# Input projection on a fixed five-engine order, and an output projection 512 columns wide, in a three-mixer decoder layer

## The chip, the cores and the metric

The kernel runs on one core of a Trainium2 chip. The metric is the device time of one execution in microseconds, the median of several runs; lower is better. Engines are named as in the profile: PE (TensorE matmul) and PEld (its weight load), DVE (VectorE), ACT (ScalarE), POOL (GpSimd), SP (SyncE, here only a queue that issues DMAs).

## The reference

One decoder layer, SEQ 1024, D_MODEL 1024, all in float32 (cut to what matters here):

```python
ada = silu(c) @ w_ada + b_ada
sh1, sc1, g1, sh2, sc2, g2 = split(ada, 6)
xn = modulate(rmsnorm(x, norm1), sh1, sc1)
z = xn @ w_in
a_u, a_v, b_x, b_g, c_q, c_k, c_v, z_gate = split(z)
out_a = gelu(a_u) * spatial_gating(layernorm(gelu(a_v)))
out_b = rg_lru(causal_conv(b_x)) * gelu(b_g)
out_c = dilated_attention(c_q, c_k, c_v)
gates = sigmoid(z_gate)
merged = gates[0] * (out_a @ p_a) + gates[1] * (out_b @ p_b) + gates[2] * (out_c @ p_c)
x = x + g1 * (merged @ w_out)
x = x + g2 * ffn(modulate(rmsnorm(x, norm2), sh2, sc2))
out = rmsnorm(x, final_norm)
```

a_u, a_v, b_x, b_g, c_q, c_k and c_v are 768 columns wide each, z_gate 3072. w_in therefore has 8448 columns.

## The kernel before

Every float32 product is made of three float32r matmuls: a high part and a low part of both operands, and of the four products the one of the two low parts is left out. The high part of a weight tile is a copy that rounds, on ACT (L116), the low part a subtraction (L117) on DVE or POOL. The projection works with a two by two block scheme of seven products instead of eight (`ORDER`): each product multiplies one of A11, A12, S1 to S4, A22 (blocks or sums of blocks of the weights) with one of B11 to T4 (blocks or sums of the activations, made once), and adds to one of four PSUM banks x, y, z and w. Three of the products use bank x and two bank z, in this order: A11 to x, A12 to y, S1 to z, S2 to x, S3 to x, A22 to w, S4 to z. Behind A11, S2 and S3 ACT copies x out (L161, L165, L167); DVE adds or subtracts behind A12, S3, A22 and S4 (L163, L168, L170, L172).

A **unit** (`unit_ws`, L176 to L194, matmul L191) makes two blocks of 128 output columns for all 1024 tokens: seven products of 12 matmuls of 512 columns. There are 25 units in the stretch of the profile that is called the projection here: one for the last two blocks of b_x, three each for b_g, a_u, c_q and c_k, twelve for the gates. c_v and a_v are made token by token row (`project_rows`, matmul L266): three units of 14 half-products of 24 matmuls of 256 columns. Four sums of weights per unit (S1 to S4, L148) alternate between POOL and DVE, and so do the low parts.

Between the units the code issues **side work** that needs their results: bias tables for attention (`bias_tables`, L595), the RG-LRU (`recurrence`, six tiles; matmuls L650, sigmoids L651), spatial gating (`spatial_gating`, six tiles; matmuls L709, L715), the head copies and stores of q and k (`post_q`, `post_k`; copies L754 and L766), and twelve late quarters of the ada vector (`late`). Loads of this work stand on SP's queue among those of the weights. The order on each engine is not that of the code: the program is built with a scheduler that simulates a timeline and places instructions by it, from all units and side work at once.

Later, after attention, the merge multiplies the mixers' outputs with p_a, p_b, p_c and the gates (L1106, with L1110 and L1111 on DVE), and w_out follows in two halves of 512 tokens, each in four chunks of 256 columns; for each chunk, four groups of 24 matmuls run one after another, each in one PSUM bank (L1145), and DVE multiplies with g1 and adds x (L1148, L1149). Then the second norm, its transposes and the FFN follow, for which the same `unit_ws` is used.

## Time and profile before

| | |
|---|---|
| runs | median of 3: 2006.84 us (2004.11 to 2011.18) |
| profiled execution | 2004.11 us, span of its instructions 2002.4 us, mean granted TensorE clock 0.98 |
| PE, DVE, ACT, POOL busy | 94%, 65%, 45%, 43% of the span |
| set-up, to 92.7 us | ada, norm, activation blocks |
| projection with its side work | 92.7 to 829.9 us |
| attention and merge | to 1224.3 us |
| w_out | to 1319 us |
| FFN and final norm | to the end |

The profile comes from one execution. A line number with L is a line of the kernel. "Idle before <- X" is the time in which an engine stood still ahead of an instruction, and what ended it. The granted clock is the clock that TensorE was given in a stretch, as a share of 2.4 GHz; its other level is 1.2 GHz. A matmul's record is longer than the distance to the next one, since matmuls are pipelined.

### The profile page before, as it was taken

What the parts mean: (1) busy time and instruction counts of PE and PEld (TensorE: products, weight loads), DVE (VectorE), ACT (ScalarE), POOL (GpSimd) and SP (SyncE); (2) the same over time, 40 slices, a digit from 0 to 9 for tenths busy, and PEclk for the clock granted to TensorE, in tenths of its full rate; (3) what the DMA queues carried; (4) which work ended last, traced back from release to release, by engine and by line L of the source; (5) the groups of instructions that cost most, each with busy time, mean ns of one, the idle gap of its engine ahead of it and who ended that gap; (6) DMA issues with size and microseconds to landing.
All of it is one profiled execution on the core that took longest, in us unless ns stands there. A gap on an engine that the chain in (4) does not pass through costs nothing. (4 is left out here: it accounts for less than half of the span.)

```text
span 2002.4 us, 27413 instructions
## 1 busy us (share of the span) xinstructions
PE 1887.5 (94%) x9503; PEld 1535.3 (77%) x9503; DVE 1300.0 (65%) x2171; ACT 896.7 (45%) x1638; POOL 857.1 (43%) x1133
## 2 busy tenths in 40 slices
PE   6889999899898989999899999998999999999997
PEld 5658998667676767778778777986787887877886
DVE  5776566477645764455556767669867666656787
ACT  5246456463643334544444433345443443334544
POOL 5453445355354334244655666456444444400002
PEclk9899999999998999999999999999999999999999
DMA  9232344347877654877876545422424333467674
GB/s 317 74 117 93 127 135 149 101 143 224 273 222 208 202 166 145 233 180 172 192 164 166 150 139 209 132 90 76 156 97 143 119 100 111 142 245 235 218 225 176
DMA packets 269994, 328.66 MB, mean 164 GB/s; under 512 B 17583, under 2 KB 196899, under 8 KB 269856
## 3 DMA queue, kind: packets, MB, share of 16 engines
q1 hardware_dynamic: 228848, 213.97, 36.0%
q10 hardware_dynamic: 33744, 87.18, 12.2%
q0 software_dynamic: 7264, 25.77, 5.2%
q8 instruction: 74, 1.21, 0.3%
q14 instruction: 64, 0.52, 0.1%
HBM read 238.64 MB, written 88.22 MB: 163 GB/s over the span
## 5 line engine op out<-in xcount | busy, mean ns | idle before, releaser
L191 PE MATMUL g<-xs,wh 128*128 128x512 f32 x2520 | 807.8, 402 | 41.9 <-DVE ot L168 11.1
L191 PEld LDWEIGHTS g<-xs,wh 128*128 128x128 f32 x2520 | 477.1, 191 | 169.6 <-DVE ot L168 12.8
L191 PE MATMUL g<-xs,wl 128*128 128x512 f32 x1260 | 499.7, 399 | 0.1
L117 POOL TENSOR_TENSOR wl<-st,wh 128x512 fp32r<-128x512 f32 x153 | 239.5, 1568 | 312.5 <-ACT wh L116 285.3
L116 ACT ACTIVATE wh<-raw 128x512 fp32r<-128x512 f32 (+2 forms) x341 | 202.1, 607 | 353.7 <-PE g L191 88.9
L191 PEld LDWEIGHTS g<-xs,wl 128*128 128x128 f32 x1260 | 239.8, 190 | 59.5 <-issue 3.4
L117 DVE TENSOR_TENSOR wl<-raw,wh 128x512 fp32r<-128x512 f32 (+2 forms) x240 | 186.5, 783 | 120.0 <-ACT wh L116 119.6
L116 ACT ACTIVATE wh<-st 128x512 fp32r<-128x512 f32 x215 | 133.4, 628 | 264.4 <-PE g L191 168.2
L117 POOL TENSOR_TENSOR wl<-raw,wh 128x512 fp32r<-128x512 f32 (+2 forms) x101 | 137.0, 1358 | 171.4 <-ACT wh L116 160.9
L148 POOL TENSOR_TENSOR st<-raw 128x512 f32<-128x512 f32 x102 | 156.6, 1539 | 119.4 <-DVE wl L117 90.6
L888 PE MATMUL gp<-oT,wh 128*128 128x512 f32 x512 | 169.7, 412 | 0.9 <-DVE ot L172 0.9
L266 PE MATMUL g<-wh,xs 128*128 128x256 f32 x672 | 126.1, 288 | 0.0
L958 ACT ACTIVATE pm<-pm,stat 128x128 f32<-128x128 f32 (+1 forms) x192 | 89.0, 465 | 51.6 <-DVE stat L955 51.1
L266 PEld LDWEIGHTS g<-wh,xs 128*128 128x128 f32 x672 | 105.0, 190 | 3.8 <-issue 3.7
L888 PEld LDWEIGHTS gp<-oT,wh 128*128 128x128 f32 x512 | 89.4, 191 | 21.8 <-issue 9.0
L1353 PE MATMUL g<-wh,wl 128*128 128x512 f32 x264 | 104.3, 395 | 0.0
L1353 PE MATMUL g<-wl,wh 128*128 128x512 f32 x264 | 104.2, 395 | 0.0
L1371 POOL TENSOR_TENSOR ms<-ms 128x1 f32<-128x1 f32 x8 | 3.6, 446 | 235.1 <-ACT junk L1370 235.0
L888 PE MATMUL gp<-oT,wl 128*128 128x512 f32 x256 | 101.9, 398 | 0.0
L1353 PE MATMUL g<-wh 128*128 128x512 f32 x264 | 94.1, 395 | 8.2 <-ACT wh L116 8.2
L266 PE MATMUL g<-wl,xs 128*128 128x256 f32 x336 | 95.4, 284 | 0.0
L955 DVE CUSTOM_DVE_ANT_0 pm<-sl,bt 128x128 f32<-128x128 f32 (+1 forms) x192 | 64.0, 378 | 47.8 <-PE sl L950 47.8
(296 smaller groups left out, 3454.1 us busy)
## 6 DMA issues: line engine op xcount, KB each, us to landing
raw<-in_w_in_dram SPq DMA_DIRECT2D x66, 512.0 KB, 5.0
raw<-in_f_wdown_dram SPq DMA_DIRECT2D x77, 256.0 KB, 5.6
adaw<-in_w_ada_dram SPq DMA_DIRECT2D x48, 256.0 KB, 6.0
g_scr<-ot ACTq DMA_DIRECT2D x24, 512.0 KB, 3.8
raw<-in_w_ada_dram SPq DMA_DIRECT2D x24, 512.0 KB, 3.6
qk<-q_scr POOLq DMA_DIRECT2D x12, 1024.0 KB, 6.4
qk<-k_scr POOLq DMA_DIRECT2D x24, 512.0 KB, 10.1
raw<-g_scr SPq DMA_DIRECT2D x24, 512.0 KB, 3.5
```

The costliest lines, as they stand in the source:

```text
L116: act.activation(h, src, AF.Copy)
L117: l_eng.tensor_tensor(l, src, h.bitcast(F32), op=OP.subtract)
L148: engs[int(name[1]) - 1].tensor_tensor(s_, src.get(x_) if isinstance(x_, str) else x_, src.get(y_) if isinstance(y_, str) else y_, op=op)
L191: pe.matmul(banks[bk], a[:, k, :], b, start=(fresh and j == 0), stop=(j == 11), skip_group_check=True)
L266: pe.matmul(banks[t2][bk][:, 256 * i:256 * i + 256], a[:, sl], b[:, k % 2, :], start=(fresh and i == 0 and j == 0), stop=(j == 11), skip_g ...
L888: pe.matmul(pt, a_[:, k % g, :], b_, start=(j == 0), stop=(j == 3 * n - 1))
L955: dve.tensor_tensor_reduce(out=pm[:, of:of + n], in0=sb[:, of:of + n], in1=bt[:, cfg, 256 - n:], scale=1.0, scalar=3e38, op0=OP.add, op1=O ...
L958: act.activation(pm[:, of:of + n], pm[:, of:of + n], AF.Exp, scale=-1.0, bias=stt[:, cfg, 0, idx:idx + 1], accum_out=stt[:, cfg, 1, idx:id ...
L1353: pe.matmul(bank, a_[:, sl], b_, start=(start and j == 0), stop=(j == 2), skip_group_check=True)
L1371: pool.tensor_tensor(ms[:, 0:1], ms[:, 0:1], ms[:, 1:2], op=OP.add)
```

## The change

From the three b_g units on, the projection is written as a fixed order for all five engines (the scheduler is switched off for PE, ACT, DVE, POOL and SP up to the end of the projection). A **slot** is one product (for the token-row units one half-product). The class `Stream` sorts all steps by slot: a unit's weights are loaded 12 slots ahead (`LOAD`), the sum and the high part are made 5 slots ahead (`LA`), the low part 4 slots ahead (`LB`), then come the slot's matmuls (L295), then one step of each of two queues of side work (`feed`), which are now generators that yield between steps, then the evacuation. The addition behind S3 comes one slot after ACT's copy. All low parts and all sums of weights are on DVE (L258, L252), the high parts on ACT (L254). The loads of side work go from SP's queue to POOL's. The first tap of the recurrence's convolution and its square move from DVE to ACT, the low parts of k from POOL to DVE. The late ada vectors are made in 48 steps of 512 columns with three buffers of their own (96 steps of 256 before). The gate units are placed between the others, so that side work has units to go along with. w_out has two chunks of 512 columns with the loop over k outside and four PSUM banks side by side, in a pool of their own. The core of the diff:

```diff
+    LA, LB, LOAD = 5, 4, 12
+
+    class Unit:
...
+            def first():
+                bl = blocks()
+                if name in formed:
+                    x_, op, y_ = formed[name]
+                    bl[name] = ring_tmp(shape)
+                    dve.tensor_tensor(bl[name], bl[x_], bl[y_], op=op)
+                it["h"] = ring.tile([P] + shape, F32R, tag="wh", bufs=8, name="wh")
+                act.activation(it["h"], bl[name], AF.Copy)
+
+            def second():
+                it["l"] = ring.tile([P] + shape, F32R, tag="wl", bufs=8, name="wl")
+                dve.tensor_tensor(it["l"], blocks()[name], it["h"].bitcast(F32), op=OP.subtract)
...
+    def evac_steps(wn, banks, m0, m1):
+
+        if wn == "S3":
+            act.activation(m1[0], banks["x"], AF.Copy)
+            z_ = banks["z"]
+            return [(1, lambda: dve.tensor_tensor(m1[1], z_, m1[0], op=OP.add))]
+        unit_evac(wn, banks, m0, m1)
+        return []
...
+    def feed(*queues):
+        for q in queues or (side, rest):
+            while q:
+                if next(q[0], StopIteration) is not StopIteration:
+                    break
+                q.popleft()
+
+    class Stream:
...
+        def add(self, u):
+            for it in u.items:
+                it["pos"] = self.n + it["rel"]
+            self.todo += [(max(0, self.n - LOAD), 0, u.load)]
+            self.todo += [(max(0, it["pos"] - LB), 1, it["second"]) for it in u.items]
+            self.todo += [(max(0, it["pos"] - LA), 0 if it["pos"] < LA else 2, it["first"]) for it in u.items]
+            self.todo += [(self.n + i, 3, mm) for i, (mm, _) in enumerate(u.slots)]
+            self.todo += [(self.n + i, 5, evac) for i, (_, evac) in enumerate(u.slots)]
+            self.n += len(u.slots)
...
+        for i in range(3):
+            fetch(i)
+        for _ in range(3):
+            yield
+        for i, (a, h, k) in enumerate(order):
+            fetch(i + 3)
...
+    phase(["bt"], lambda: side.append(bias_tables(side_pool["bt"])))
+    for j in (0, 2):
+        stream.add(project(COL["bg"], z_scr["bg"], AF.Gelu_apprx_tanh, j))
+    phase(["rg"], queue_recurrence)
+    stream.add(project(COL["bg"], z_scr["bg"], AF.Gelu_apprx_tanh, 4))
+    for j in range(3):
+        stream.add(project_rows(j))
+        gate_units(2 * j)
+    for j in range(0, KW, 2):
+        stream.add(project(COL["au"], z_scr["au"], AF.Gelu_apprx_tanh, j))
+    phase(["sg"], lambda: side.append(spatial_gating(side_pool["sg"])))
+    gate_units(6, 8, 10, 12, 14, 16)
+    phase(["hl", "ad"], lambda: rest.append(late(side_pool["ad"])))
+    for name in "qk":
+        for j in range(0, KW, 2):
+            stream.add(project_heads(name, j, lambda: side_pool["hl"]))
+    gate_units(18, 20)
...
-            for c in range(4):
-                cs = slice(256 * c, 256 * c + 256)
...
-                for i in range(4):
-                    pt = gbank("go")
...
+            for c in range(2):
+                cs = slice(HALF * c, HALF * c + HALF)
+                pts = [pwo.tile([P, HALF], F32, tag="wo", bufs=4, name="go") for _ in range(4)]
+                for k in range(KD):
...
+                    for i, pt in enumerate(pts):
                         sl = slice(i * P, i * P + P)
+                        for j, (a_, b_) in enumerate(((mh, wh), (mh, wl), (ml, wh))):
+                            pe.matmul(pt, a_[:, sl], b_, start=(k == 0 and j == 0), stop=(k == KD - 1 and j == 2))
+                for i, pt in enumerate(pts):
+                    tmp = ring_tmp([HALF])
+                    dve.tensor_tensor(tmp, pt, g1b[:, cs], op=OP.mult)
                     dve.tensor_tensor(x2[i][:, cs], x2[i][:, cs], tmp, op=OP.add)
```

How instructions now stand, at three places. The first is PE's order in the projection around a unit's products S2 and S3, which share a bank (here a `g` with one number). Before, in the spatial gating's stretch: S2 ends in bank g_4540, then two matmuls into another unit's bank, two of side work (L709), and a product of a third unit (g_4412); S3's first matmul into g_4540 stands 18 rows behind S2's last.

```order
L191 MATMUL g_4540<-xs_1010,wh_4593 128x512
L191 MATMUL g_4540<-xs_1009,wl_4594 128x512
L191 MATMUL g_4540<-xs_1017,wh_4593 128x512
L191 MATMUL g_4540<-xs_1018,wh_4593 128x512
L191 MATMUL g_4540<-xs_1017,wl_4594 128x512
L191 MATMUL g_4634<-xs_1039,wh_4630 128x512 x2
L709 MATMUL m_4141<-vs_4128,wst_4124 128x512
L709 MATMUL m_4144<-vs_4128,wst_4124 128x512
L191 MATMUL g_4412<-xs_882,wh_4484 128x512
L191 MATMUL g_4412<-xs_883,wh_4484 128x512
```

Now, at the corresponding stretch, S2's last matmuls into g_4972, two of side work (L884, the same matmuls as L709), and S3's first ones into g_4972. 23 units have this order; in 13 of them nothing stands between S2 and S3, in the others one side step as here.

```order
L295 MATMUL g_4972<-xs_1009,wl_4943 128x512
L295 MATMUL g_4972<-xs_1017,wh_4914 128x512
L295 MATMUL g_4972<-xs_1018,wh_4914 128x512
L295 MATMUL g_4972<-xs_1017,wl_4943 128x512
L884 MATMUL m_5077<-vs_4933,wst_5052 128x512
L884 MATMUL m_5080<-vs_4933,wst_5052 128x512
L295 MATMUL g_4972<-xs_1023,wh_4947 128x512
L295 MATMUL g_4972<-xs_1024,wh_4947 128x512
L295 MATMUL g_4972<-xs_1023,wl_4968 128x512
```

What moved: the other unit's product that stood between the two is gone, so S3 follows the copy of the bank (L165) directly.

The second is ACT's order in the recurrence, ahead of L165. Before, L165 stood between splits, and the recurrence's activations (L651, L654, L655) behind it:

```order
L565 ACTIVATE ot<-ot 128x1024
L116 ACTIVATE wh<-st 128x512
L165 ACTIVATE ot<-g 128x512
L560 DMA au_scr<-ot 128x1024
L116 ACTIVATE wh<-raw 128x512
L651 ACT_TABLE_LOAD
L651 ACTIVATE rr<-m,cols_382 128x512 x2
L654 ACT_TABLE_LOAD
L654 ACTIVATE aa<-rr,spn 128x1024
```

Now (L789 is the same sigmoid as L651, L254 the split's high part, L677 a gelu of a finished unit):

```order
L254 ACTIVATE wh<-raw 128x512
L789 ACT_TABLE_LOAD
L789 ACTIVATE rr<-m,cols_382 128x512 x2
L254 ACTIVATE wh<-raw 128x512
L789 ACTIVATE ii<-m,cols_382 128x512 x2
L165 ACTIVATE ot<-g 128x512
```

What moved: a step of the recurrence stands directly ahead of L165. Three units have it so.

The third is PE's order where the merge ends and w_out begins. Before, the merge's groups (L1106) all end before the first matmul of w_out (L1145):

```order
L1106 MATMUL gp_11478<-oT_10995,wh_11278 128x512
L1106 MATMUL gp_11478<-oT_10996,wh_11278 128x512
L1106 MATMUL gp_11478<-oT_10995,wl_11279 128x512
L1145 MATMUL go_11538<-wh_11520,mh_11226 128x256
L1145 MATMUL go_11538<-wl_11521,mh_11226 128x256
L1145 MATMUL go_11538<-wh_11520,ml_11227 128x256
```

Now (L1370 is the merge, L1407 w_out, with its four banks go_11500 to go_11503):

```order
L1370 MATMUL gp_11313<-oT_10971,wh_11245 128x512
L1370 MATMUL gp_11313<-oT_10970,wl_11246 128x512
L1407 MATMUL go_11500<-wh_11506,mh_11205 128x512
L1407 MATMUL go_11500<-wl_11507,mh_11205 128x512
L1407 MATMUL go_11501<-wh_11506,mh_11205 128x512
L1407 MATMUL go_11501<-wl_11507,mh_11205 128x512
L1407 MATMUL go_11502<-wh_11506,mh_11205 128x512
L1407 MATMUL go_11502<-wl_11507,mh_11205 128x512
L1407 MATMUL go_11503<-wh_11506,mh_11205 128x512
L1407 MATMUL go_11503<-wl_11507,mh_11205 128x512
L1370 MATMUL gp_11325<-oT_10258,wh_11251 128x512
L1370 MATMUL gp_11325<-oT_10259,wh_11251 128x512
```

What moved: w_out's matmuls begin between the last groups of the merge.

## Rows read from the trace of the kernel before

**Rows 1.** Page, part 1: busy us, share of the span, instructions

```profile
PE 1887.5 (94%) x9503; PEld 1535.3 (77%) x9503; DVE 1300.0 (65%) x2171; ACT 896.7 (45%) x1638; POOL 857.1 (43%) x1133
```

**Rows 2.** By stage: window, us; busy (x) of PE, PEld, DVE, ACT, POOL; clock, DMA, GB/s

```profile
92.70:831.00 738.30, 686.84 (x3302) 551.35 (x3301) 458.28 (x619) 355.12 (x494) 321.94 (x256) 0.97 0.53 165
...
1224.30:1319.00 94.70, 94.70 (x792) 94.70 (x793) 53.89 (x87) 30.75 (x51) 38.97 (x35) 1.00 0.47 162
1319.00:1400.00 81.00, 76.49 (x352) 61.87 (x350) 70.50 (x67) 40.60 (x68) 51.89 (x41) 1.00 0.22 68
```

**Rows 3.** PE groups of the projection: x count, busy us, mean ns, idle before

```profile
L191 PE MATMUL g<-xs,wh 128*128 128x512 f32 x1400 | 458.7, 409 | 32.4 <-DVE ot L168 11.1 <-ACT ot L165 9.0 <-ACT wh L116 5.7
...
L650 PE MATMUL m<-xv,bd 128*128 128x512 f32 x48 | 25.6, 641 | 5.9 <-DVE xv L644 4.0 <-ACT rr L651 1.9
...
L950 PE MATMUL sl<-qk 128*128 128x256 f32 (+1 forms) x8 | 1.1, 280 | 0.0
```

**Rows 4.** Timeline of PE at full pace: start us, us

```profile
744.01 0.63 PE L191 MATMUL g<-xs,wh 128*128 128x512 f32 x2
...
744.72 0.63 PE L191 MATMUL g<-xs,wh 128*128 128x512 f32 x2
```

**Rows 5.** Timeline of PE: four of the 20 idles of 0.6 us and more

```profile
105.80 0.97 PE L191 MATMUL g<-xs,wh 128*128 128x512 f32 x3 [2.29 <-ACT xs L116]
...
640.93 1.22 PE L191 MATMUL g<-xs,wh 128*128 128x512 f32 x2 [5.69 <-ACT wh L116]
...
666.49 0.73 PE L191 MATMUL g<-xs,wh 128*128 128x512 f32 x2 [2.16 <-ACT ot L165]
...
826.80 0.73 PE L191 MATMUL g<-xs,wh 128*128 128x512 f32 x2 [2.82 <-DVE ot L168]
```

**Rows 6.** Granted clock around two of these idles (columns as in rows 2)

```profile
636.00:647.00 11.00, 6.07 (x16) 4.99 (x17) 5.44 (x5) 4.47 (x8) 5.92 (x5) 0.56 0.70 229
665.00:669.00 4.00, 2.51 (x11) 2.06 (x12) 2.12 (x4) 2.70 (x4) 1.40 (x1) 1.00 0.47 142
```

**Rows 7.** Split and sum groups of the projection on POOL and DVE

```profile
L117 POOL TENSOR_TENSOR wl<-st,wh 128x512 fp32r<-128x512 f32 x90 | 136.0, 1516 | 181.8 <-ACT wh L116 159.5 <-PE m L709 12.2 <-DMA q_scr<-ot 10.0
...
L148 POOL TENSOR_TENSOR st<-raw 128x512 f32<-128x512 f32 x59 | 92.9, 1580 | 68.3 <-DVE wl L117 40.8 <-DMA raw<-in_w_in_dram 21.6 <-DVE st L148 1.4
...
L117 DVE TENSOR_TENSOR wl<-raw,wh 128x512 fp32r<-128x512 f32 (+1 forms) x63 | 57.6, 915 | 46.9 <-ACT wh L116 46.9
...
L117 POOL TENSOR_TENSOR wl<-raw,wh 128x512 fp32r<-128x512 f32 (+1 forms) x33 | 49.2, 1493 | 81.9 <-ACT wh L116 77.1 <-DMA oT<-oa_scr 4.7
```

**Rows 8.** Line L117, whole kernel: ns min/median/max, first and last start

```profile
L117 DVE TENSOR_TENSOR wl<-st,wh x62: 671/683/1789, 83.0 to 1954.5; 128x512 fp32r<-128x512 f32 x62
```

**Rows 9.** Timelines of PE and ACT around the idle at 666.49

```profile
663.94 0.39 PE L191 MATMUL g<-xs,wl 128*128 128x512 f32 x1
...
665.32 0.63 ACT L116 ACTIVATE wh<-st 128x512 fp32r<-128x512 f32 x1 [2.85 <-DVE st L148]
665.85 0.58 ACT L165 ACTIVATE ot<-g 128x512 f32<-128x512 f32 x1
```

**Rows 10.** Head copies of the projection's q units on ACT

```profile
L766 ACT ACTIVATE hlp<-ot 128x1024 f32<-128x1024 f32 x6 | 12.4, 2070 | 8.9 <-issue 5.2 <-DMA q_scr<-hlp 3.7
```

**Rows 11.** Timeline of ACT at a table load

```profile
426.34 1.28 ACT L654 ACT_TABLE_LOAD   x1
...
427.64 1.15 ACT L654 ACTIVATE aa<-rr,spn 128x1024 f32<-128x1024 f32 x1
```

**Rows 12.** Timeline of PE at the merge's end: first and last of three idles

```profile
1214.90 0.73 PE L1106 MATMUL gp<-oT,wh 128*128 128x512 f32 x2 [1.71 <-DVE st L1110]
...
1222.56 0.74 PE L1106 MATMUL gp<-oT,wh 128*128 128x512 f32 x2 [1.70 <-DVE st L1110]
```

**Rows 13.** Page, part 6: DMA issues, KB each, us from issue to landing

```profile
adaw<-in_w_ada_dram SPq DMA_DIRECT2D x48, 256.0 KB, 6.0
...
qk<-k_scr POOLq DMA_DIRECT2D x24, 512.0 KB, 10.1
```

More of the change, by code (lines that the diff above doesn't have):

```diff
@@ new lines, in evac_steps, with stream_ws, blocks, mm @@
+    def evac_steps(wn, banks, m0, m1):
[5 more added lines that the diff above has]
+        return []
+    def stream_ws(gb, tcomb, views, ot, post):
+        u = Unit(views, [KD, P])
+        bl, banks, out_ = {}, {}, []
+        def blocks():
+            if not bl:
+                (r0, r1) = u.raws
+                bl.update(A11=r0[:, :4, :], A12=r0[:, 4:, :], A21=r1[:, :4, :], A22=r1[:, 4:, :])
+            return bl
+        for i, (wn, tn, bk) in enumerate(ORDER):
+            it = u.part(i, wn, blocks, [4, P])
+            def mm(wn=wn, tn=tn, bk=bk, it=it):
+                fresh = bk not in banks
+                if fresh:
+                    banks[bk] = gb(bk)
+                j = 0
+                for k in range(4):
+                    th, tl = tcomb[tn][k]
+                    for a, b in ((it["h"], th), (it["h"], tl), (it["l"], th)):
+                        pe.matmul(banks[bk], a[:, k, :], b, start=(fresh and j == 0), stop=(j == 11),
+                                  skip_group_check=True)
+                        j += 1
+            def evac(wn=wn):
+                if not out_:
+                    out_.extend(ot())
+                m0, m1 = out_
+                later = evac_steps(wn, banks, (m0[:, 0], m0[:, 1]), (m1[:, 0], m1[:, 1]))
+                return later + (post(m0, m1) if wn == "S4" else [])
+            u.slots.append((mm, evac))
+        return u
@@ L238, in feed, with __init__, call @@
                 q.popleft()
+    class Stream:
+        def __init__(self):
+            self.todo, self.n, self.later, self.at = [], 0, {}, 0
+        def add(self, u):
[7 more added lines that the diff above has]
+            self.n += len(u.slots)
+        def call(self, marks=()):
+            todo = self.todo + [(s_, -1, f) for s_, f in marks]
+            todo += [(s_, 4, None) for s_ in range(self.n)]
+            for s_, kind, f in sorted(todo, key=lambda x_: x_[:2]):
+                if kind == 4:
+                    feed()
+                    for g in self.later.pop(s_, ()):
+                        g()
+                elif kind == 5:
+                    for d, g in f():
+                        self.later.setdefault(s_ + d, []).append(g)
+                else:
+                    f()
+            while side or rest:
+                feed()
+            for s_ in sorted(self.later):
+                for g in self.later[s_]:
+                    g()
     def run_fed(unit):
@@ L793, in trunk, with mark, phase, enter @@
         for q in range(2):
             scale_cols(mod2, "norm2", q)
+    sched = ctx.enter_context(ExitStack())
+    sched.enter_context(tc.manual_schedule(engines={mybir.EngineType[e] for e in "PE,Activation,DVE,Pool,SP".split(",")}))
+    stream = Stream()
+    marks = []
+    pools = ExitStack()
+    side_pool = {}
+    def mark(f):
+        marks.append((stream.n, f))
+    def phase(open_, queues):
+        def enter():
+            while side or rest:
+                feed()
+            pools.close()
+            for n in open_:
+                side_pool[n] = pools.enter_context(tc.tile_pool(name=n, bufs=1))
+            queues()
+        mark(enter)
@@ new lines, in gate_units, with queue_recurrence @@
+    def gate_units(*js):
+        for j in js:
+            stream.add(project(COL["z"], g_scr, AF.Sigmoid, j))
+    def queue_recurrence():
+        res = []
+        side.append(recurrence_consts(side_pool["rg"], res))
+        side.extend(recurrence(side_pool["rg"], ct, res) for ct in range(KW))
+    phase(["bt"], lambda: side.append(bias_tables(side_pool["bt"])))
+    for j in (0, 2):
+        stream.add(project(COL["bg"], z_scr["bg"], AF.Gelu_apprx_tanh, j))
+    phase(["rg"], queue_recurrence)
@@ L814, in load_head @@
         return qp, qn, kh, kl, bt
-    project(COL["z"], g_scr, func(AF.Sigmoid), (), 16, 20)
-    head0 = load_head(0)
-    project(COL["z"], g_scr, func(AF.Sigmoid), (), 20, 3 * KD)
+    phase(["hd"], queue_heads)
+    gate_units(22)
+    stream.call(marks)
+    head0 = heads[0]
+    sched.close()
     x1.close()
```

366 lines of the change are left out of this document (223 added, 143 removed).

## Prediction

> **What bounds the kernel now.** I read the page first: TensorE works through 94% of the span [rows 1], so time can only come from its idle, its half-speed stretches and the pace of its matmuls. The table by stage says where. In the projection (92.70 to 831) PE is busy 686.84 of 738.30 us, so 51.5 us idle, and its granted clock is 0.97; w_out is 94.70 busy of 94.70 [rows 2]. So the change can act on the projection, on the hand-over into w_out, and on w_out's own pace.
>
> The matmul groups of the projection give its floor [rows 3]. At full clock three 512-wide matmuls start every 0.71 us (744.01 to 744.72), 0.235 each [rows 4]. A unit of the column form has 84, there are 25: 2100 x 0.2347 = 492.9 us. The row form's 1008 matmuls of 256 columns (three units of 14 half-products of 24) go at w_out's pace, 94.70 / 792 = 0.120 each [rows 2]: 121.0 us. The side work's eight groups, from L650 (25.6 us) to L950 (1.1), hold 61.0 us of records [rows 3]; these overlap (a 512-wide record lasts 0.40 at a pace of 0.235), so I take 50. Floor 664. The stage lasts from 92.7 to the end of its last matmul at 829.9, 737.2 us: **73 us of overhead**.
>
> The timeline of PE shows the overhead's form: 20 idles of 0.6 us or more, first at 105.80, last at 826.80, 49 us in all, most of them ended by an evacuation on ACT or DVE or a late split (5.69 at 640.93 behind ACT's wh) [rows 5]. Around some the granted clock drops to the lower of its two levels, 1.2 instead of 2.4 GHz: 0.56 in 636 to 647; around the 2.16 us idle at 666.49 it stayed 1.00 [rows 5, 6]. A mean clock of 0.97 over 738 us is 22 us of lost clock, some of it in idle; I take 18 as lost work. 51.5 + 18 is 69.5 of the 73; the rest are gaps too short to list.
>
> **The change, part by part.** *Splits and sums on VectorE.* POOL gives up 90 + 33 low parts and 59 sums of this stage. They took it 1.5 to 1.6 us each [rows 7]; DVE has a median of 0.683 for the same split [rows 8]. DVE gains 182 x 0.684 = 124 us, loses about 16 (six first conv taps and six squares of 1024 columns go to ACT, at twice 0.68) and some 10 (late ada in 48 wide steps instead of 96 narrow ones), and gets back some 30 where POOL ran beside it: its own 63 low parts from raw averaged 0.915 [rows 7], 0.23 over the median, and I allow the same for its other two-input work. From 458 [rows 2] it goes to about 526 of 720 us, 73%: not the bound. A split now stands four slots (4 x 12 x 0.235 = 11.3 us) ahead of its product, so waits such as the 5.69 us one should go.
>
> *The fixed order.* In before, the two products that share bank x, S2 and S3, are kept apart by another unit's product, so ACT's evacuation of x between them is covered. In the new order S3 follows S2 directly or after a short piece of side work, in 23 units. The bare price is read at 666.49: S2's last matmul starts at 663.94 and lasts 0.39, L165 takes 0.58, and PE starts 0.06 after L165's end [rows 5, 9]. With a start latency of the same 0.06 and the 0.16 by which a record outlasts its pace, a clean wait costs 0.16 + 0.06 + 0.58 + 0.06, about 0.9. What stands ahead of L165 in ACT's queue adds to it. From the order: ten have nothing ahead that matters (0.9); three in the recurrence have L789's two sigmoids directly ahead, which first wait for the side matmuls behind S2 (two more activations, about 2.0); three beside the q heads have a head copy (2.07 for one L766 [rows 10]) and its stores, about half covered by the product (2.5 with the issues); seven have small side steps in between (1.2). Sum 9 + 6 + 7.5 + 8.4 = **31 us**, 1.35 a unit. The lower bound is 23 x 0.9 = 21 (nothing below: the data dependence is there); the upper one is the rival below.
>
> *Start and seams.* The first four of the 20 idles (105.80 to 127.53) belong to the tail of the set-up and stay, 6 us; the stream's first four products have no lead, 4 x (0.58 + 0.68) = 5 more, by L165's time and the split's. Draining the side queues where a phase changes lets two or three side steps run at once: 3. For causes that I can't place (the row form's first slots after a column unit, the q phase) I set three idles like the one of 2.16, 6.5 us, and once the clock that 636 to 647 lost, 0.44 x 11 = 4.8 [rows 6]: 11. **Overhead after: 11 + 31 + 3 + 11 = 56 instead of 73, gain 17.** Side loads move from SP's queue to POOL's software queue; SP then issues only weights, twelve slots (34 us) ahead, and POOL has little else left. I cost this at nothing as long as they land in time; what covers it is the steps' lead of two or three slots.
>
> *ACT.* It gains six taps and six squares, 14 us at twice L165's 0.58, on 355 of 738 [rows 2]: half busy. Its queue is in order, though, and the new order has 30 table loads in this stage's. A load took 1.28, and the next activation began 0.02 after its end (426.34 to 427.64) [rows 11]; so a switch costs 1.28 here. The Trainium skill ("ScalarE: Activation LUTs", What ACT_TABLE_LOAD costs) puts a drain of 1380 ns on top, 2.66 us a switch. The trace disagrees at this row. By that rule the sum would carry 1.38 us for each load that delays an L165.
>
> *w_out.* 768 matmuls at 0.120 are 92.2; 384 of 512 columns at 0.2347 are 90.1: gain 2. Its matmuls may now fill the merge's tail, where PE waits for DVE's L1110, three idles, the first of 1.71 at 1214.90, the last of 1.70 at 1222.56, 4.6 together [rows 12]: up to that much more. But the four banks now end together, in the last 12 matmuls, and DVE then needs 8 operations of 128x512, 5.5 us at 0.68, where before only the last bank's two of 256 columns were left, at most 1.4 at that rate. The half-1 rows come some 4 later into a stretch (1319 to 1400) in which DVE is busy 70.50 of 81 [rows 2]. Net 2 + 4.6 - 4 = **3**, rounded up, from -2 to +7.
>
> **Sum.** 17 + 3 = 20 off the profiled execution's 2004.1 us (span 2002.4) gives 1984; that execution lies 2.7 under the median of 2006.8, so a median of **1987**.
>
> **Rivals.** *Bare waits.* If ACT is always in time, 23 waits cost 21, the start 6, and the 14 of seams and unplaced idles vanish: overhead 27, gain 46, with w_out up to 7 more, so 1954 to 1975, about 1962. For: half of the units have nothing else in front of L165. Against: already in before, L165 ended 9.0 us of L191's idle [rows 3].
>
> *L165 queues behind the side work (ends slower).* Place: ACT, S2 to S3. Were two head copies with their issues to stand ahead in the six q and k units (5 us), and a table load with sigmoids or square roots in eight more (3.5), the waits would be 30 + 28 + 9 x 1.5 = 72, 41 more than in my sum; some of those over 2 us would also draw the low clock, as the wait at 640.93 did. Time 1987 + 41 = 2028, a little less if only part of it holds. Gain and loss meet where overhead is 76 = 25 + 23 w, at w = 2.2 us; it is slower by over 0.3% from 2.5. For: at 666.49 most of the 2.16 us was a split ahead of L165, which itself waited 2.85 us for a sum on DVE [rows 9]. Against: the side steps are spread, one a slot of 2.8 us.
>
> *The late ada loads starve (no gain, or slower).* 48 chunks rotate through three buffers, one a slot. A landing of 6.0 us, as the ada loads of the sync queue have, lets three pass in 7, less than three slots (8.5). On the software queue k's loads took 10.1 [rows 13]: three in 11, 0.85 us too slow a slot, 41 us over 48 slots, of which DVE's lead of 11 is free. The time would be 1987 + 30 = 2017; it decides from a landing of about 7.6. The k loads are strided, the ada rows whole 2 KB runs, so 6 is nearer. The Trainium skill ("SBUF — State Buffer", SBUF: two separate sides) warns that a DMA issued by GpSimd can be held up while a DVE instruction has the shared port; no row here shows it.
>
> *A table switch costs more than its load.* With some twelve loads ahead of an L165, 1.38 each, 17 us: 2004. The row speaks against it; the page named above is its only support.
>
> *The gain is given back later*, in attention's first loads (head 0 is loaded one unit ahead, 20 us, not two) or in the FFN: about 2003.
>
> **How the numbers follow.** A measurement of this kernel can tell about 0.3%, 6 us, from no change. My forecast (waits of 1.0 to 1.8 us, 1976 to 2003) has 0.50; bare waits 0.22; L165's queue 0.13; ada loads 0.09; table switches 0.02; given back 0.04. Faster (under 2000.8) takes 0.45 of the forecast's, all of the bare waits' and 0.02 of the ada loads' chance, 0.69; slower (over 2012.8) L165's queue and half of the ada loads, 0.18; 0.13 is left for the same. The range from 1958 to 2014 leaves out most of the slower rivals and a tail of the best case.
>
> **What would show it.** Right: about 23 idles on PE ended by ACT's L165, 0.9 to 2.5 us long, and hardly another over 2; a clock of 0.99 in the stage; DVE's low parts near 0.68 with no mean of 0.9; POOL almost idle there; the first matmul of attention near 815 instead of 830.75; 384 matmuls of w_out at 0.235 and no wait for L1110 ahead of them. Wrong: idles in front of S3 of 3 us and more, DVE waiting for adaw, PE waiting for a split that DVE or ACT brought late, or a stage no shorter than 737.

## The result, and the profile after

The changed kernel takes 1981.81 us (median of 4, 1980.75 to 1988.19) against 2005.47 for the kernel before: a ratio of 0.9893, 95% interval 0.987 to 0.9917. Run again beside the fifth to seventh experiments it took 1987.11 (ratio 0.9905, 0.9877 to 0.9932). So it is faster by 17 to 24 us, about 1%. The profiled execution took 1982.27.

The first lines of the page of the changed kernel (as [rows 1]); POOL fell from 857 to 634 us, PE's share rose by one point.

```profile
span 1980.6 us, 26351 instructions
...
PE 1874.4 (95%) x9119; PEld 1508.4 (76%) x9119; DVE 1287.9 (65%) x2259; ACT 899.5 (45%) x1644; POOL 633.8 (32%) x1067
```

The table by stage of the changed kernel (columns as in [rows 2]): the projection up to 805, and the first 30 us of attention.

```profile
91.80:805.00 713.20, 676.52 (x3300) 543.40 (x3298) 464.50 (x734) 356.21 (x498) 102.21 (x191) 0.99 0.54 171
805.00:835.00 30.00, 26.09 (x115) 20.59 (x115) 16.86 (x60) 12.73 (x38) 11.01 (x47) 0.89 0.92 223
```

The projection runs from 91.5 (91.8 here) to 804.2, 712.7 us instead of 737.2, with 36.7 instead of 51.5 us idle and a clock of 0.99. DVE is busy 464.50, hardly more than the 458.28 before [rows 2], though it now makes every split and sum. Attention's first product (here always the first matmul into gp) starts at 806.0 instead of 830.75, 25 us earlier; but attention then begins with idle PE (3.9 of these 30 us) and a clock of 0.89.

PE's and DVE's groups of the changed kernel's projection (as [rows 3, 7]):

```profile
L295 PE MATMUL g<-xs,wh 128*128 128x512 f32 x1344 | 435.9, 405 | 31.1 <-ACT ot L165 21.7 <-DVE ot L269 9.4
...
L258 DVE TENSOR_TENSOR wl<-st,wh 128x512 fp32r<-128x512 f32 x120 | 82.1, 684 | 18.8 <-ACT wh L254 18.6
...
L258 DVE TENSOR_TENSOR wl<-raw,wh 128x512 fp32r<-128x512 f32 x90 | 62.0, 694 | 28.0 <-ACT wh L254 28.0
```

PE no longer waits for a split. Its idle ahead of L295 has two names, L165 (21.7) and L269 (9.4). The low parts are at 0.684 and 0.694, those from raw at 0.915 before. The timeline of PE shows the kinds of wait (as [rows 5]):

```profile
442.50 0.72 PE L295 MATMUL g<-xs,wh 128*128 128x512 f32 x2 [0.69 <-ACT ot L165]
...
514.49 0.73 PE L295 MATMUL g<-xs,wh 128*128 128x512 f32 x2 [1.62 <-DVE ot L269]
...
653.85 1.22 PE L295 MATMUL g<-xs,wh 128*128 128x512 f32 x2 [3.08 <-ACT ot L165]
...
798.99 1.22 PE L295 MATMUL g<-xs,wh 128*128 128x512 f32 x2 [4.64 <-DVE ot L269]
```

The first is the bare wait between S2 and S3, eleven times 0.69. The third is one of two in the q units. The second and the fourth come from the addition L269 behind S3, for which the next product in bank z, S4, waits.

The bare wait, on PE and on ACT in the changed kernel (as [rows 9]):

```profile
307.14 0.40 PE L295 MATMUL g<-xs,wl 128*128 128x512 f32 x1
308.23 0.73 PE L295 MATMUL g<-xs,wh 128*128 128x512 f32 x2 [0.69 <-ACT ot L165]
```

```profile
307.58 0.60 ACT L165 ACTIVATE ot<-g 128x512 f32<-128x512 f32 x1 [1.44 <-PE g L295]
```

S2's last matmul ends at 307.54 by its record, L165 begins 0.04 later and takes 0.60, PE starts 0.05 after it. At full pace the next matmul would have started at 307.375, so the unit loses 0.86 us; the row calls 0.69 of it idle.

### The profile page after: what moved, and what is told of

Read it like the earlier page. It is cut to its first block, busy times and chain, and to the rows that moved or that the text cites. A ratio compares the mean times of both kernels' runs of the same rounds, so it can differ in the third digit from the quotient of the medians.

```text
span 1980.6 us, 26351 instructions
## 1 busy us (share of the span) xinstructions
PE 1874.4 (95%) x9119; PEld 1508.4 (76%) x9119; DVE 1287.9 (65%) x2259; ACT 899.5 (45%) x1644; POOL 633.8 (32%) x1067
## 4 chain that ended last, share of the span: by engine, by line
PE 72%; DMA 9%; DVE 6%; issue 6%; POOL 3%; ACT 2%; SPq 1%; ACTq 0%; DVEq 0%; POOLq 0%
PE g L191 18%; PE g L295 18%; PE gp L1152 7%; PE g L334 6%; PE g L1615 6%; PE go L1407 4%; PE sl L1214 3%; DMA adaw<-in_w_ada_dram 2%; PE g L215 2%; PE tp L1258 1%; PE o L1287 1%; PE gp L1370 1%; PE m L788 1%; DMA res<-x_scr 1%; PE o L1290 1%
## 5 line engine op out<-in xcount | busy, mean ns | idle before, releaser
L295 PE MATMUL g<-xs,wh 128*128 128x512 f32 x1344 | 435.9, 405 | 31.1 <-ACT ot L165 21.7
L191 PE MATMUL g<-xs,wh 128*128 128x512 f32 x1176 | 367.6, 394 | 9.5 <-DVE up L168 2.7
L295 PEld LDWEIGHTS g<-xs,wh 128*128 128x128 f32 x1344 | 251.3, 190 | 107.8 <-ACT ot L165 32.1
L116 ACT ACTIVATE wh<-raw 128x512 fp32r<-128x512 f32 (+2 forms) x251 | 147.2, 601 | 274.2 <-issue 58.8
L191 PEld LDWEIGHTS g<-xs,wh 128*128 128x128 f32 x1176 | 220.3, 188 | 63.0 <-ACT xs L116 3.1
L295 PE MATMUL g<-xs,wl 128*128 128x512 f32 x672 | 267.9, 399 | 0.0
L191 PE MATMUL g<-xs,wl 128*128 128x512 f32 x588 | 230.4, 393 | 0.0
L117 DVE TENSOR_TENSOR wl<-raw,wh 128x512 fp32r<-128x512 f32 (+2 forms) x180 | 129.8, 727 | 84.2 <-ACT wh L116 84.0
L295 PEld LDWEIGHTS g<-xs,wl 128*128 128x128 f32 x672 | 127.8, 190 | 31.2
L117 POOL TENSOR_TENSOR wl<-st,wh 128x512 fp32r<-128x512 f32 x63 | 104.0, 1651 | 144.3 <-ACT wh L116 139.4
L117 POOL TENSOR_TENSOR wl<-raw,wh 128x512 fp32r<-128x512 f32 (+2 forms) x71 | 92.3, 1301 | 123.1 <-ACT wh L116 108.4
L254 ACT ACTIVATE wh<-st 128x512 fp32r<-128x512 f32 x120 | 75.2, 627 | 120.6 <-DVE st L252 120.4
L191 PEld LDWEIGHTS g<-xs,wl 128*128 128x128 f32 x588 | 110.5, 188 | 24.9
```

The lines of the kernel that those rows point to most:

```text
L116: act.activation(h, src, AF.Copy)
L117: l_eng.tensor_tensor(l, src, h.bitcast(F32), op=OP.subtract)
L191: pe.matmul(banks[bk], a[:, k, :], b, start=(fresh and j == 0), stop=(j == 11), skip_group_check=True)
L254: act.activation(it["h"], bl[name], AF.Copy)
L295: pe.matmul(banks[bk], a[:, k, :], b, start=(fresh and j == 0), stop=(j == 11), skip_group_check=True)
```

## The experiments

My theory after the result: the fixed order, with its lead of four slots, is what shortened the projection; the engine of the splits matters little; what overhead is left is the wait of S3 and S4. The first rival: the splits, taken from POOL, are the gain. The second: w_out is. The kernel before ran beside each group, at 2004.4 to 2006.3.

### 1. The scheduler switched on again

```diff
-    sched.enter_context(tc.manual_schedule(engines={mybir.EngineType[e] for e in "PE,Activation,DVE,Pool,SP".split(",")}))
```

> The changed kernel's code with the projection's order left to the timeline scheduler again; all else as in the change (splits on DVE, side loads on POOL's queue, w_out 512 wide, splits no longer tied to a lead of slots). Theory (the fixed order with its lead is what shortens the projection): most of the 24.8 us by which attention starts earlier is lost, idles of 2 to 6 us come back, time 1998 to 2010, clearly slower than the changed kernel's 1981.8. Rival (it is the splits on DVE, free of POOL): attention still starts near 806 us, time 1978 to 1988.

Measured: 1979.84 (ratio 0.9874, 0.9838 to 0.9911), the changed kernel's time. The theory fell here: the order that the scheduler makes of the same code is as good, so neither the gain nor what overhead is left hangs on the order being a fixed one. It has other waits, mostly the addition L269 (L295's group of this kernel's projection):

```profile
L295 PE MATMUL g<-xs,wh 128*128 128x512 f32 x1344 | 436.9, 406 | 25.6 <-DVE ot L269 15.3 <-ACT ot L267 5.7 <-ACT ot L165 4.7
```

Its projection is shorter (90.9 to 793.1), but from attention's first product to the end of w_out it takes 494.8 us where the changed kernel takes 487.8.

### 2. Six of the eleven splits and sums of a unit back on POOL, in the fixed order

```diff
-                    dve.tensor_tensor(bl[name], bl[x_], bl[y_], op=op)
+                    (pool if name in ("S1", "S3") else dve).tensor_tensor(bl[name], bl[x_], bl[y_], op=op)
...
-                dve.tensor_tensor(it["l"], blocks()[name], it["h"].bitcast(F32), op=OP.subtract)
+                (dve if name in ("A12", "S2", "A22") else pool).tensor_tensor(it["l"], blocks()[name], it["h"].bitcast(F32), op=OP.subtract)
```

> The changed kernel, its order fixed, but sums S1 and S3 and four of each unit's seven low parts on POOL as before. Theory (the order with its lead matters, the engine of the splits hardly): POOL needs 6 x 1.3 to 1.6 = 8 to 10 us of a 19.7 us unit, four slots ahead, so the waits stay those of the changed kernel; DVE's two-input work gets slower, some units lose a little: 1982 to 1990. Rival (the splits on DVE are the gain): PE waits for splits again, 1995 to 2005.

Measured: 1992.46 (0.9937, 0.9907 to 0.9966), 5 to 11 us more than the changed kernel, between the two forecasts. The projection itself was only 3 us longer, 92.9 to 808.6, though its splits were slower (groups of this kernel's projection):

```profile
L295 PE MATMUL g<-xs,wh 128*128 128x512 f32 x1344 | 436.8, 406 | 32.0 <-ACT ot L165 17.6 <-DVE ot L269 14.4
...
L258 POOL TENSOR_TENSOR wl<-st,wh 128x512 fp32r<-128x512 f32 x90 | 129.7, 1443 | 159.2 <-ACT wh L254 155.2 <-PE g L295 3.6
...
L258 DVE TENSOR_TENSOR wl<-raw,wh 128x512 fp32r<-128x512 f32 x60 | 59.8, 997 | 28.5 <-ACT wh L254 28.4
```

POOL takes 1.44 us for a low part, DVE's low parts from raw take 1.0 instead of 0.69, and PE still waits for no split, only for L165 and L269. PE's idle in the projection is 36.4 us, against 35.9 in the changed kernel from its first matmul to its last; and in the second profile of the changed kernel (the eighth, below) the projection took 717.5 us, longer than the 715.7 here. So in the fixed order the lead hides the slow splits: that half of the theory held. Of the 5 to 11 us by the medians the trace puts hardly any into the projection.

### 3. S3 in a bank of its own

```diff
+        if wn == "S3" and "v" in banks:
+            dve.tensor_tensor(m1[0], banks["v"], m0[1], op=OP.add)
+            dve.tensor_tensor(m1[1], banks["z"], m1[0], op=OP.add)
+            return []
         if wn == "S3":
...
+            bk = "v" if wn == "S3" else bk
             it = u.part(i, wn, blocks, [4, P])
```

> The changed kernel with product S3 in a PSUM bank of its own: DVE adds ACT's copy of x to it, instead of S3 adding to bank x after ACT has copied x out; DVE then adds bank z at once. Theory (what is left of the overhead is the wait of S3 for L165, 21.7 us in 21 idles, and of S4 for the addition L269, 9.4 us in 5): the first goes wholly, of the second all but the last unit's 4.6, with two low-clock spells around the idles at 654 and 679 (about 3 us): 1981.8 - 21.7 - 4.8 - 3 = 1952, range 1950 to 1962. Rival (the wait only moves: DVE or ACT are late in the same places, next at S4 or in front of a split): 1970 to 1982, with idles of about 0.7 us elsewhere.

Measured: 1957.08 (0.9763, 0.9736 to 0.979). PE's group and the window of this kernel's projection:

```profile
L300 PE MATMUL g<-xs,wh 128*128 128x512 f32 x1344 | 434.2, 404 | 8.1 <-DVE ot L268 6.3 <-ACT ot L161 1.8
```

```profile
91.80:774.70 682.90, 670.10 (x3301) 543.20 (x3299) 475.24 (x748) 337.44 (x460) 102.72 (x191) 1.00 0.56 177
```

No idle ends with L165 any more, and 8.1 us are left in front of L300 (the changed kernel's L295). The projection is 682.9 us long, 30 less than the changed kernel's; 12.8 of 682.90 are idle. So S3's and S4's waits, and the low clock around the longest of them (in the changed kernel 0.83 from 650 to 660 and 0.54 from 798 to 804.3), were most of the overhead that was left. 25 us of the 30 reach the end; ahead of attention's first product PE now idles 5.89 us, 1.75 in the changed kernel.

### 4. w_out as before

```diff
-            for c in range(2):
-                cs = slice(HALF * c, HALF * c + HALF)
+            for c in range(4):
+                cs = slice(256 * c, 256 * c + 256)
...
```

> The changed kernel with w_out as before: four chunks of 256 columns, one bank after another. Theory (w_out's share: from the start of the merge to the FFN's first L191 wait the trace shows 5.0 + 1.5 us less than before, but attention took 7.4 us longer up to the merge's start because the order of the merge's groups moved with it): the net of w_out is 2 to 7 us, 1984 to 1989. Rival (w_out gives nothing net, the whole gain is the projection's): 1980 to 1983.

Measured: 1995.80 (median of 10, 0.9961, 0.9944 to 0.9977): 9 to 14 us more than the changed kernel, above both forecasts. The traces give w_out less. Before, from the last matmul of attention's second product (line L1023) to the last of w_out:

```profile
L1023 PE MATMUL o<-st,v x360: 272/273/324, 853.5 to 1179.9; 128*64 128x128 f32 x180
...
L1145 PE MATMUL go<-wh,ml x256: 278/283/363, 1224.6 to 1319.0; 128*128 128x256 f32 x128
```

And in the changed kernel:

```profile
L1287 PE MATMUL o<-st,v x360: 272/273/473, 834.4 to 1162.0; 128*64 128x128 f32 x180
...
L1407 PE MATMUL go<-wh,ml x128: 387/389/628, 1185.6 to 1293.8; 128*128 128x512 f32 x128
```

1179.9 to 1319.0 is 139.1 us, 1162.0 to 1293.8 is 131.8: 7.3 less (from start to start). The same stretch takes 139.3 us in the fourth kernel, and 131.4 and 131.8 in the fifth and the eighth below, so this part is steady. The rest of the 9 to 14 is spread over the stages of a profile that was itself 6.6 over its median; I can't place it.

### 5 to 8. The parts in the kernel before, and the change once more

The fifth kernel is the kernel before with the change's w_out, the sixth the kernel before with all sums and low parts of the projection on DVE, the seventh has both, the eighth is the changed kernel again. The edit of the sixth:

```diff
+        one = dict(engs=(dve,) * 4, l_engs=(dve,)) if proj[0] else {}
+        get = weight_combos(r0[:, :4, :], r0[:, 4:, :], r1[:, :4, :], r1[:, 4:, :], [4, P], **one)
...
+        parts = [weight_combos(*[r[:, 2 * p:2 * p + 2, :] for r in raws], [2, 256], (dve,) * 4, (dve,)) for p in range(2)]
```

> The kernel before with the change's w_out alone (two chunks of 512 columns, four banks). Theory (w_out is a part of its own worth about 7 us, as the traces show between the end of attention and the end of w_out, 131.8 us in the changed kernel against 139.1): 1995 to 2000 against 2005.2, the projection as before. Rival A (worth 14, the difference of the medians of the changed kernel and of the one with the old w_out): 1989 to 1993. Rival B (worth nothing by itself, the merge's idles stay): 2003 to 2007.

> The kernel before, its scheduler and its code order kept, with all sums and low parts of the projection on DVE. Theory (putting two thirds of them back on POOL cost the changed kernel 10.6 us, so this is a part that pays by itself): attention starts 8 to 14 us earlier, 1991 to 1998. Rival (with the old order PE waits for evacuations, which sit on the now fuller DVE): 2002 to 2010.

> The kernel before with both: all sums and low parts of the projection on DVE, and w_out 512 wide. Nothing of the fixed order, of the slots or of the moved loads. Theory now (the two parts make the whole gain, the fixed order none): 1979 to 1986, the changed kernel's time. Rival (the order in slots, the loads ahead and the gate units spread among the side work carry a part that the scheduler of the first experiment kept, since it started from that code order): 1988 to 1997.

> The changed kernel itself, on the same chip as the three others. If the chip doesn't matter: 1980 to 1985. If the old-w_out kernel's 14 us were partly the chip's: 1985 to 1989.

Measured, against 2004.42: the fifth 1999.32 (0.9971, 0.9954 to 0.9987), the sixth 1975.04 (0.9854, 0.9831 to 0.9878), the seventh 1964.04 (0.9795, 0.9771 to 0.982), the eighth 1987.11. So the fourth experiment's 14 us shrink to 9 beside this second measurement of the change. The fifth met its forecast and the eighth the higher of its two; the sixth and the seventh came out far below every forecast.

This is what decided the case. Two small edits of the kernel before, with its own order and its own scheduler, give 40 us; the change, which has both and the fixed order besides, gives 17 to 24. By itself w_out gives 5 and the splits on DVE 29; the 6 that both together give beyond that are within the intervals. What the change adds to these two costs about 18 to 23 us.

Two groups of DVE in the projection of the kernel before (not among the rows above), and then four of the sixth kernel (L194 is before's L191, L647 its L644):

```profile
L148 DVE TENSOR_TENSOR st<-st,raw 128x512 f32<-128x512 f32 x29 | 37.2, 1284 | 48.3 <-POOL wl L117 27.0 <-POOL st L148 21.3
...
L644 DVE SCALAR_TENSOR_TENSOR xv<-xp,cols,xv 128x1024 f32<-128x1024 f32 x18 | 29.6, 1642 | 0.4
```

```profile
L194 PE MATMUL g<-xs,wh 128*128 128x512 f32 x1400 | 454.0, 407 | 23.3 <-ACT ot L165 10.4 <-ACT wh L116 4.5 <-DVE ot L168 4.4
...
L117 DVE TENSOR_TENSOR wl<-raw,wh 128x512 fp32r<-128x512 f32 (+1 forms) x93 | 66.8, 726 | 32.0 <-ACT wh L116 29.6 <-PE m L402 1.6 <-PE g L194 0.7
...
L647 DVE SCALAR_TENSOR_TENSOR xv<-xp,cols,xv 128x1024 f32<-128x1024 f32 x18 | 23.0, 1278 | 0.1
L148 DVE TENSOR_TENSOR st<-st,raw 128x512 f32<-128x512 f32 x29 | 22.1, 761 | 0.4
```

With POOL out of the way the convolution's taps fall from 1.64 to 1.28 us, the chained sums from 1.28 to 0.76, and those no longer stand still for POOL (48.3 us before, 0.4 now). Ahead of L194 PE idles 23.3 us, ahead of L191 it was 32.4 [rows 3]; attention's first product starts at 794.0, 37 us earlier than before and 12 to 16 earlier than in the changed kernel. Of the 37, 5 lie ahead of the projection (it begins at 87.7 instead of 92.7), 21 are less idle of PE in it (29.4 instead of 50.6 us), and 11 are matmuls that took less time, with a clock of 0.98 instead of 0.97.

### 9 and 10. What about POOL costs the time

The ninth kernel is the sixth with additions on POOL that nobody needs, in the first half of the projection; the tenth is the kernel before with only the sums on DVE.

```diff
+            for _ in range(2 if dmy and proj[0] and wn != "A22" else 0):
+                pool.tensor_tensor(dmy[1].rearrange("p (a b) -> p a b", a=2), dmy[0].rearrange("p (a b) -> p a b", a=2), wh.bitcast(F32)[:, :2, :], op=OP.add)
```

> The kernel of the sixth experiment (before, all sums and low parts of the projection on DVE) with useless additions on POOL in the first half of the projection, up to the spatial gating: 12 of 256 columns for each unit, each reading a high part that ACT has made, nobody reading what they write. They give POOL about the load that the splits gave it, without anything waiting for them. Theory (POOL harms by slowing DVE's two-input work, 0.68 to 0.9 and 1.28 to 1.64): a good part of that half's gain goes, 1982 to 1990, and the taps of the convolution take 1.5 us or more again. Rival (POOL harms because a sum or split on it takes 1.3 to 1.6 us and stands in the chain that PE waits for): 1972 to 1979.

> The kernel before with the sums of the projection on DVE and the low parts alternating between DVE and POOL as they did. Theory (the sums are what is late: S1 on POOL, then S2, then S4, each ahead of ACT's high part): most of the sixth experiment's gain stays, 1976 to 1984. Rival (the low parts on POOL, the last step ahead of a product and two thirds of POOL's work, are what costs): 1990 to 2002.

Measured: the ninth 2004.22 (0.9997, 0.9983 to 1.0011), the tenth 2004.70 (0.9994, 0.9975 to 1.0012). Each loses the whole gain; I had expected up to half of it for the ninth, and for the tenth its rival came true in kind, 3 us above its range.

Groups of the ninth kernel's projection (L197 is before's L191, L189 the useless additions of the column units, beside 72 more in the row units, L656 the taps), and who waited for L189 (us, times):

```profile
L197 PE MATMUL g<-xs,wh 128*128 128x512 f32 x1389 | 456.6, 411 | 40.8 <-DVE ot L168 17.8 <-ACT ot L165 12.3 <-ACT wh L116 4.0
...
L189 POOL TENSOR_TENSOR dmyo<-dmya,wh 128x256 f32<-128x256 f32 x84 | 89.9, 1071 | 26.7 <-ACT wh L116 20.8
...
L117 DVE TENSOR_TENSOR wl<-raw,wh 128x512 fp32r<-128x512 f32 (+1 forms) x93 | 72.8, 790 | 29.6 <-ACT wh L116 27.5 <-PE g L197 2.0
...
L148 DVE TENSOR_TENSOR st<-st,raw 128x512 f32<-128x512 f32 x29 | 27.1, 936 | 0.4
L656 DVE SCALAR_TENSOR_TENSOR xv<-xp,cols,xv 128x1024 f32<-128x1024 f32 x18 | 27.1, 1503 | 0.1
...
L168 DVE TENSOR_TENSOR ot<-g,ot 128x512 f32<-128x512 f32 x31 | 21.2, 683 | 21.2 <-ACT ot L167 21.1
```

```profile
  ACT wh L116: 16.6, 7
```

The first half by the table of stages, in the sixth kernel and in the ninth (the two windows don't hold quite the same work, 1854 and 1816 matmuls):

```profile
92.00:430.00 338.00, 333.19 (x1854) 279.91 (x1852) 239.85 (x341) 193.90 (x264) 16.33 (x30) 0.99 0.40 131
```

```profile
92.00:450.00 358.00, 334.27 (x1816) 278.93 (x1815) 282.14 (x331) 190.33 (x260) 180.42 (x185) 0.97 0.36 117
```

Nobody reads what POOL makes here, and yet the taps are back at 1.50, low parts from raw at 0.79 and chained sums at 0.94, as means over a stage of which only half is loaded. DVE's additions out of PSUM (L168) stay at 0.683, but come late. PE's idle that ends with L168 is 17.8 us, not 4.4: 4.77 in the last unit, much as in the sixth kernel (4.37), and 5.59 and 7.43 in the loaded half. Ahead of the 7.43, DVE's queue holds slow work in front of L168:

```profile
362.40 1.74 DVE L656 SCALAR_TENSOR_TENSOR xv<-xp,cols,xv 128x1024 f32<-128x1024 f32 x1
364.06 1.21 DVE L148 TENSOR_TENSOR st<-raw 128x512 f32<-128x512 f32 x1
365.19 1.74 DVE L656 SCALAR_TENSOR_TENSOR xv<-xp,cols,xv 128x1024 f32<-128x1024 f32 x1
...
367.46 0.68 DVE L168 TENSOR_TENSOR ot<-g,ot 128x512 f32<-128x512 f32 x1
```

Ahead of the 5.59 (at 172.91) the queue was as full, but mostly of small operations of the recurrence at their ordinary speed. The first matmul of the spatial gating starts at 487.4 instead of 456.3. One thing makes the size of the effect unclear: the additions read ACT's high parts, so ACT waited 16.6 us for buffers that POOL had not yet read.

The tenth kernel's groups (L194 is before's L191):

```profile
L194 PE MATMUL g<-xs,wh 128*128 128x512 f32 x1400 | 457.2, 409 | 30.3 <-DVE ot L168 9.9 <-ACT wh L116 5.4 <-ACT ot L167 4.7
...
L148 DVE TENSOR_TENSOR st<-raw 128x512 f32<-128x512 f32 x59 | 55.5, 945 | 27.9 <-POOL wl L117 16.6 <-DMA raw<-in_w_in_dram 10.9
```

With the low parts alone on POOL, DVE's sums take 0.945 and wait 16.6 us for a low part on POOL, and PE's idle is 30.3, near the 32.4 of before. So the low parts on POOL are enough to cost the 29 us; whether the sums on POOL alone would be enough too, no run shows. Two ways show in the traces: DVE's work with two inputs in SBUF gets slower, and DVE waits for POOL in the chain. How much each costs was not separated.

### 11 and 12. Versions that beat both kernels

The eleventh kernel is the seventh with S3 in a bank of its own; the twelfth is the third with the last gate unit written behind the fixed order, for the scheduler to place.

> The seventh experiment's kernel (before with DVE splits and w_out 512 wide, no fixed order) and S3 in a PSUM bank of its own. Theory (the scheduler covers most waits of S3 for L165, but not all: 0.72, 8.56 and, through L167 and L168, 1.95 and 1.48 were left): 1964 less 5 to 12 us, 1950 to 1959, as good as the fixed order with its own bank (1957) or better. Rival (a fifth bank of six per unit leaves the scheduler fewer to overlap units with): 1962 to 1975.

> The third experiment's kernel (fixed order, S3 in a bank of its own), but the last gate unit is taken out of the stream and written behind the end of the fixed order, where the scheduler places it together with attention's first work. Theory (the fixed order loses some 7 to 9 us at its end: the last unit's S4 and attention's first products wait behind one another on ACT and DVE, and the clock is low around it; the third experiment took 488 us from attention's first product to the end of w_out, the seventh 479): 1957 less 4 to 9, 1948 to 1953. Rival (the loss sits in attention's own loads, not in the last unit's order): 1955 to 1962.

Measured: the eleventh 1956.92 (0.9766, 0.9728 to 0.9805), the twelfth 1956.21 (0.9762, 0.9723 to 0.9802). The eleventh's 7 over the seventh are within its forecast, though not quite clear of noise, and it stands level with the third: once S3 has its own bank, the fixed order and what came with it bring nothing over the old order, and cost nothing. So the own bank gives 25 to 30 us in the new code and 7 in the old; the difference is what the change had lost against the seventh. The twelfth is a miss, and its rival came true. Its last unit waits much as before, two rows of PE's timeline and one of ACT's:

```profile
774.03 1.22 PE L191 MATMUL g<-xs,wh 128*128 128x512 f32 x2 [4.19 <-DVE ot L168]
...
780.70 0.69 PE L1161 MATMUL gp<-oT,wh 128*128 128x512 f32 x2 [1.29 <-DVE ot L172]
```

```profile
768.58 1.21 ACT L116 ACTIVATE oT<-oT 128x512 fp32r<-128x512 f32 x2 [4.65 <-DMA oT<-oa_scr]
```

ACT's copy behind S3 (L167, 771.77) stands behind splits of the merge's operand oT, for whose load ACT stood still for 4.65 us; L168 follows on DVE. So the scheduler too puts work that waits for a load ahead of the last unit's copy. What the hand-over from the projection to attention costs without that was not run.

## Why the prediction was right, and where it was not

**The number** was right, 1987 against 1981.8 and 1987.1, and so was the sign, in part by luck. The floor and the overhead held: 49 us are left over the floor of 664, I had 56. So by the two profiles the projection gave 24.5 us, where the sum had 17. But from its first product to the last matmul of its second product (L1023, now L1287) attention takes 7 us more, 356.0 instead of 349.1, which the sum had at nothing, and the two cancel. It loses them at its start: in its first 30 us PE makes 119 matmuls, 152 before.

**The splits: here the reasoning fell short.** The step "Splits and sums on VectorE" counted what DVE gains and loses, found it "not the bound", and gave the move no place in the sum; the end of the waits was credited to the four slots of lead. The runs show two ways to the same end. In the old order the move alone is worth 29 us (sixth); in the fixed order the lead hides POOL's slow splits, as the step had it, so there the move is worth 5 to 11 by the medians and next to nothing in the projection's trace (second). DVE's relief, "some 30", was far too small: DVE is busy 464.50 us, where the sum had 526. What I missed is that an engine busy at 62% still sets the time when its queue is in order: a slow split ahead of an evacuation delays PE. The longest idle of the projection before, 6.03 us, shows it, with both ways in one place: a sum that waits for POOL's low part, and then takes 1.77 as the low part behind it does, both ahead of L168:

```profile
348.44 1.77 DVE L148 TENSOR_TENSOR st<-st,raw 128x512 f32<-128x512 f32 x1 [1.19 <-POOL wl L117]
350.14 1.77 DVE L117 TENSOR_TENSOR wl<-raw,wh 128x512 fp32r<-128x512 f32 x1
...
357.46 0.68 DVE L168 TENSOR_TENSOR ot<-g,ot 128x512 f32<-128x512 f32 x1
```

```profile
358.20 1.22 PE L191 MATMUL g<-xs,wh 128*128 128x512 f32 x2 [6.03 <-DVE ot L168]
```

The row at 666.49 with a split ahead of L165 [rows 9], late from a sum on DVE, said the same of ACT's queue, and I used it only for a rival.

**The fixed order's price** was right in kind and place. L165 ended 21.7 us of idle, with 0.16 more for each of 21 waits by the pace about 25; I had 31. The bare wait costs 0.86, I had 0.9. The q units' waits came in two of three units, 3.08 and 2.81 us; the q copy stood ahead of L165, and had itself waited, in the first of them for DVE (shown here), in the second 0.76 us for a store:

```profile
651.28 2.03 ACT L933 ACTIVATE hlp<-ot 128x1024 f32<-128x1024 f32 x1 [0.73 <-DVE adaa L975]
...
653.22 0.58 ACT L165 ACTIVATE ot<-g 128x512 f32<-128x512 f32 x1
```

What I did not see is that this price is as large as the whole gain: the third kernel gets 25 to 30 us back with one more bank.

**A term that was missing**: S4 waits for L269. I gave "The addition behind S3" no price. The step is put behind a slot's side work, so eight operations of the spatial gating pass it on DVE:

```profile
511.70 2.13 DVE L868 TENSOR_SCALAR vs<-vs,stats 128x128 f32<-128x128 f32 x8
513.75 0.68 DVE L269 TENSOR_TENSOR ot<-g,ot 128x512 f32<-128x512 f32 x1
```

S4's waits cost 9.4 us, 4.64 of them in the last unit. There the spatial gating is long over, and it is ACT's queue: the copy behind S3 (L267) stands behind a split of the merge's operand, which waits for its load:

```profile
796.29 0.63 ACT L116 ACTIVATE oT<-oT 128x512 fp32r<-128x512 f32 x1 [2.88 <-DMA oT<-oa_scr]
...
797.24 0.58 ACT L267 ACTIVATE ot<-g 128x512 f32<-128x512 f32 x1
```

**Terms that were too large**: the start and the seams between phases. Of 11 + 3 + 11 us the timeline shows 2.4 at the start, and outside L165 and L269 only two more idles over 0.6 us (1.69 and 0.78).

**w_out** was forecast at 3, from -2 to +7. Its own stretch is 7.3 us shorter by the traces, where the sum had 2 + 4.6; the stages behind it take 686.8 us instead of 683.4, where it had 4 more, but they run from 681 to 690 over the profiles of this case. By itself in the kernel before w_out gives 5.1, by the fourth kernel's medians more. The merge's tail filled as I said: w_out's first matmul now starts at 1182.4, 39 us ahead of the merge's last (1221.0).

**The rivals.** *Given back later*, 0.04, happened in part: attention begins at 806 with 0.89 of the clock and some 4 us of idle, and from its first product to the end of w_out the changed kernel takes 487.8 us, as before (488.2), though w_out is 7 shorter. It was not head 0's load: PE's idle there ended with the splits of the merge's operands, which waited for their loads, and with the last unit's evacuation. *The ada loads* did not starve; on the software queue they land in 5.1 us, well under the 7.6 that I had worked out as the limit:

```profile
adaw<-in_w_ada_dram POOLq DMA_DIRECT2D x48, 256.0 KB, 5.1
```

DVE waited 7.9 us in all for them (L975 3.9, L973 4.0), and no idle of PE of 0.3 us or more ended with them. *A table switch* cost its 1.28 and no more: behind the load at 797.84 the next activation began at 799.13. That a drain comes on top, as the Trainium skill has it ("ScalarE: Activation LUTs", What ACT_TABLE_LOAD costs), this row does not show either.

## What to carry to other kernels

Before an order is rewritten, try the one-line moves inside the old one: here the splits on one engine gave 29 us and two edits together 40, the new order with both 17 to 24. Two products that add to one PSUM bank, with a copy of it between them, cost PE the copy's whole latency wherever nothing else stands between; a further bank and an addition give that back. When a forecast's number is right, the parts still need a run each: here the projection gave 7 us more than forecast, and attention, which the forecast left as it was, lost as much.

## What the runs showed of the hardware

POOL's two-input work slows DVE's two-input work even when no data connects them: with a POOL that adds a constant tile to high parts in half the stage, for nobody to read, DVE's taps of 1024 columns went from 1.278 to 1.503 us and chained sums from 0.761 to 0.936, and POOL's own additions of 256 columns took 1.07 at a minimum of 0.74. DVE's additions with an input in PSUM kept their 0.683. The Trainium skill ("SBUF — State Buffer", Who interferes with whom) says that a DVE instruction with two inputs in SBUF contends with a GpSimd instruction that reads SBUF, and that one with at most one such input, outside the 2-port perf modes, does not; these runs agree on both. I had not expected that a load on POOL, half of one stage long, would undo a gain of 29 us, even with ACT's 16.6 us of waits for its buffers in it.
